# Later remainder terms in a three-term float32r product: a conv + RG-LRU layer on one core

## The chip, the core and the metric

The kernel runs on one core of a Trainium2 chip. The engines that matter are TensorE (PE, the matmuls; its weight loads are listed as PEld), VectorE (DVE), ScalarE (ACT), GpSimd (POOL, which here issues the transfers that add into their destination) and SyncE (SP, which issues the plain transfers). The metric is the device time of one execution in microseconds (us). Before the change the median of three runs is 729.47 us (728.41 to 730.4).

## The reference

One layer of a hybrid decoder: 1024 tokens of 1024 channels, float32.

```python
mod = silu(c) @ mod_w + mod_b
shift, scale, gate = split(mod, 3)
h = rmsnorm(x, norm_g) * (1 + scale) + shift
cv, cg, cs, lx, ls = split(h @ w_in)            # five blocks of 1024 columns

v = cv * sigmoid(cg)                            # conv group
v = causal_depthwise_conv(v, dw_w, dw_b)        # 31 taps
v = silu(layernorm(v, cln_g, cln_b))
y_conv = (v @ pw2_w + pw2_b) * silu(cs)

xs = causal_depthwise_conv(lx, sc_w, sc_b)      # lru group, 4 taps
r, i = sigmoid(xs @ wr + br), sigmoid(xs @ wi + bi)   # 8 heads of 128
a = exp(-8 * r * softplus(-lam))
hs = linear_scan(a, sqrt(1 - a**2) * (i * xs))
y_lru = hs * silu(ls)

x = x + (1 + gate) * (concat([y_conv, y_lru]) @ w_out)
out = rmsnorm(x, final_g)
```

The parts that the change touches are the product `v @ pw2_w`, and the product with `w_out`: its upper half takes `y_conv`, its lower half `y_lru`.

## The kernel before

**Layout.** Channels lie on the 128 partitions and the 1024 tokens on the free axis, so a 1024 x 1024 operand is eight tiles of 128 x 1024. A matmul takes a 128 x 128 block of weights and 512 tokens.

**A product of three terms.** The matmuls run in float32r, which keeps fewer bits than float32. So each operand is split into a high part, rounded to float32r, and a remainder, and a product is the sum of three matmuls: H, high weights by high data; X, high weights by the remainder of the data; W, the remainder of the weights by high data. In names, `h` and `l` mark the two: `yha0` and `yla0`, `whiout1` and `wloout1`, `whi46` and `wlo46`. In `mm_k` and in `product` (inside `pair_products`) the three terms stand side by side for every k block: H, X, W of block 0, then of block 1, and so on, in one operation of three (or six) matmuls that asks for all four operands.

**How remainders are made.** Those of the data come mostly from VectorE (a subtraction, L405). Those of weights come from VectorE, or by `remainder`: ScalarE writes minus the high part, and a transfer issued by POOL adds the original to it from DRAM. `remainder` makes `wlo46` and `wlo47`, the remainders of the weights of the last two lru tiles, as it makes `wlopw20`, `wloout0` and `wloout1`.

**The lower half of the output, lru pairs and tiles.** `w_out`'s lower half by `y_lru` is computed first, while the conv group is still in its LayerNorm: `lru_pair` computes output tiles 0 to 5 in pairs (PSUM tiles `lp`, `lx`, `ly`; pair 2 is number 44 and 45), and the last two tiles are plain ones, number 46 and 47 (`ps46`, `ps47`), by `mm_k` over eight k blocks. Each tile is scaled by the gate into `acc0` to `acc7`; then POOL issues a transfer that adds it onto a copy of x in DRAM (`accd0` to `accd7`). Later SP loads `accd` back as `fin`, onto which the upper half of the output is added.

**The pairs of the conv group.** `pw2` and the upper half of `w_out` go two output tiles at a time: pairs 0 to 3 of each, named `pw2_0` to `out_3`. A pair is computed with seven products of half size (`pair_products`), called `1 z 2 y 3 s 4`, of sums and differences of the quarters. Product `1` is the quarter A11 by B11 (data `vha`, `vla` or `yha`, `yla` in PSUM tile `x`), `z` is A12 by B21 (`vhb`, `vlb`, tile `z`), `y` takes T1 and `4` takes T4. The data's quarters are split by `quarters`, half on ScalarE and half on VectorE. The evacuations of the PSUM tiles go to `yc` (pw2) and `fin` (out).

**Order.** All instructions are put in order by `Plan`, ahead of the run. Each operation has an engine, an assumed cost, a priority number and the operations that it must wait for, by the buffers that it reads and writes. `Plan.order` plays time forward: whenever an engine is free, it takes the ready operation with the smallest priority. So a change of what one operation reads can move many others on every engine. The order is then fixed; on the chip an engine runs its list in that order and stops at the first instruction whose inputs are not there. Most tiles of 128 x 1024 come from one pool of 47 buffers (`big`); an instruction that takes a buffer waits until the last use of the one before is over, a transfer out of it included.

Of the kernel before, what the change touches and what calls it, by code (L numbers as in the profile page):

```python
# [16 lines left out]
T = 1024  # L17
# [81 lines left out]
LWO = 0.5  # L99
LRV = ()  # L100
# [233 lines left out]
def hymba_layer(ctx: ExitStack, tc: tile.TileContext, xT, vecs, mod_w, w_first, w_in,  # L334
# [162 lines left out]
    def w_slice(s, k, nk, p_load, p_prep, first_load=(), eng="POOL", late=()):  # L497
# [6 lines left out]
        if eng == "DMA":  # L504
            remainder(p_prep, cut(lo), cut(hi), lambda: wsrc(s)[:, c, :], n, keys(hi), keys(lo))
# [11 lines left out]
    def weights(s, after=(), n=None, eng=None, where=None, late=()):  # L517
# [3 lines left out]
        w_slice(s, 0, KT, n - 2.5, n - 1.4, after, eng, late)  # L521

    def mm_k(prio, ps, s, xh, xl, k, cols, off=0, first=0, final=KT - 1, after=()):
        wh, wl = whi[s], wlo[s]
        at = LK.index(k) if s[0] == "lru" else k

        def emit():
            for lhs, rhs, last in ((wh, xh, 0), (wh, xl, 0), (wl, xh, 1)):
                for a, b in cols:
# [3 lines left out]
                              stop=(k == final and bool(last)), skip_group_check=True)  # L533
        n = sum(b - a for a, b in cols)
        rd = [(wh, at), (wl, at)]
        wr = []
        for a, b in cols:
            rd += halves(xh[k], a, b) + halves(xl[k], a, b)
            wr += halves(ps, a - off, b - off)
        return S.op("PE", 3 * sum((b - a + 32) / 2400 for a, b in cols), emit, prio, rd, wr, after=after, columns=3 * n)  # L540
# [145 lines left out]
    def pair_products(name, n, w, sets, use, orders=(ORDER7,), apart=0):  # L686
# [7 lines left out]
        def product(a, b, ps, start):  # L694
            (wh, wl), xs, made = w[a], sets[b], products[name, c]
            for j, (bh, bl) in enumerate(xs):
                def emit(j=j, bh=bh, bl=bl):
                    for lhs, rhs, t in ((wh, bh, 0), (wh, bl, 1), (wl, bh, 2)):
                        pe.matmul(half(ps, 0)(), half(*lhs)()[:, j * P:j * P + P], half(*rhs)(),  # L699
                                  start=start and j == 0 and t == 0,  # L700
                                  stop=j == KT // 2 - 1 and t == 2, skip_group_check=True)
                o = S.op("PE", 3 * (H + 32) / 2400, emit, n + 0.15 * q, [wh, wl, bh, bl],
                         [ps], columns=3 * H)
                made.append(o)
                if j == 0:
                    ops.append(o)

        for order in orders:
# [18 lines left out]
            n += apart  # L727

    def rstd(prio, sqs, a, e, ps, o, after=(), warm=(), idle=None):
# [27 lines left out]
        S.op("DVE", 0.2, lambda: dve.reciprocal(rs()[:, :nb], sd()[:, :nb]), prio, [sd], [rs])  # L757
# [986 lines left out]
```

## Time and profile before

| | |
|---|---|
| median of 3 runs | 729.47 us (728.41 to 730.4) |
| profiled execution, its own time | 730.56 us |
| its span in the profile | 728.7 us |
| granted TensorE clock, mean | 0.996 |
| TensorE busy | 718.4 us (99%), 3274 matmuls |
| VectorE, ScalarE, POOL busy | 616.9, 481.7, 171.0 us |

The span runs from the first to the last instruction that the profile lists; the execution's own time holds 1.9 us more. Rows of a timeline have the start from the beginning of the span, the length, the engine, the line of the kernel, the operation with output and inputs (buffer numbers are left out, so `vlb` stands for `vlb0` to `vlb3`), and in brackets the engine's idle time before it and what ended it. Matmuls overlap: the length shown of one with 512 columns is 0.39 us, though the next may start 0.23 us after it. So a stop of TensorE is read from the starts.

Of the work named here, the LayerNorm of the conv group and lru pair 2 lie at about 500 to 540 us, `ps46` and `ps47` up to 560, the four pairs of pw2 from 560 to 640, the four pairs of out from 634 on, the final norm and the stores after 702.

### The profile page before, as it was taken

What the parts mean: (1) busy time and instruction counts of PE and PEld (TensorE: products, weight loads), DVE (VectorE), ACT (ScalarE), POOL (GpSimd) and SP (SyncE); (2) the same over time, 40 slices, a digit from 0 to 9 for tenths busy, and PEclk for the clock granted to TensorE, in tenths of its full rate; (3) what the DMA queues carried; (4) which work ended last, traced back from release to release, by engine and by line L of the source; (5) the groups of instructions that cost most, each with busy time, mean ns of one, the idle gap of its engine ahead of it and who ended that gap; (6) DMA issues with size and microseconds to landing.
All of it is one profiled execution on the core that took longest, in us unless ns stands there. A gap on an engine that the chain in (4) does not pass through costs nothing.

```text
span 728.7 us, 9085 instructions
## 1 busy us (share of the span) xinstructions
PE 718.4 (99%) x3274; PEld 597.2 (82%) x3274; DVE 616.9 (85%) x848; ACT 481.7 (66%) x615; POOL 171.0 (23%) x172
## 2 busy tenths in 40 slices
PE   9999999999999999999999999999999999999996
PEld 8888888888888888888888888878878788878885
DVE  7999999899689998688499995999788666999646
ACT  7650679555689857957949779858874345755322
POOL 0035223443434230233220220211101101110003
PEclk9999999999999999999999999999999999999998
DMA  8945338768899997899998687998936955784006
GB/s 340 407 158 167 51 112 234 189 119 199 192 217 206 263 234 196 183 224 211 192 246 259 125 175 173 255 249 229 226 44 140 250 122 138 216 224 159 8 15 216
DMA packets 46059, 137.80 MB, mean 189 GB/s; under 512 B 5200, under 2 KB 15824, under 8 KB 45904
## 3 DMA queue, kind: packets, MB, share of 16 engines
q0 software_dynamic: 20016, 54.84, 41.8%
q1 hardware_dynamic: 24992, 81.48, 32.2%
q10 hardware_dynamic: 1008, 0.92, 0.4%
q8 instruction: 25, 0.41, 0.2%
q14 instruction: 18, 0.15, 0.1%
HBM read 79.37 MB, written 21.50 MB: 138 GB/s over the span
## 4 chain that ended last, share of the span: by engine, by line
PE 81%; issue 6%; DVE 5%; ACT 4%; DMA 2%; POOL 1%; DVEq 0%; POOLq 0%; ACTq 0%
PE ps L530 49%; PE xout L699 5%; PE first L826 5%; PE xpw L699 5%; PE ypw L699 3%; PE gate L1246 2%; PE y L674 2%; PE lp L530 1%; DMA wloout<-in_w_out_dram 1%; PE zpw L699 1%; DMA accd<-acc 1%; PE zout L699 1%; PE lx L1378 1%; ACT L386 1%; PE yout L699 1%
## 5 line engine op out<-in xcount | busy, mean ns | idle before, releaser
L530 PE MATMUL ps<-ul,whi 128*128 128x512 f32 x576 | 177.4, 389 | 0.0
L530 PE MATMUL ps<-uh,whi 128*128 128x512 f32 x576 | 177.4, 389 | 0.0
L530 PE MATMUL ps<-uh,wlo 128*128 128x512 f32 x576 | 177.2, 389 | 0.0
L530 PEld LDWEIGHTS ps<-ul,whi 128*128 128x128 f32 x576 | 108.1, 188 | 22.5
L530 PEld LDWEIGHTS ps<-uh,wlo 128*128 128x128 f32 x576 | 108.1, 188 | 22.5
L530 PEld LDWEIGHTS ps<-uh,whi 128*128 128x128 f32 x576 | 108.0, 188 | 22.3
L378 ACT CAST whi<-raw 128x1024 fp32r<-128x1024 f32 (+1 forms) x44 | 45.1, 1032 | 46.1 <-PE ps L530 28.4
L410 POOL DMA_DIRECT2D es<-cq x45 | 40.6, 902 | 129.8 <-ACT cq L386 89.6
L405 POOL TENSOR_TENSOR wlo<-raw,whi 128x1024 fp32r<-128x1024 f32 x16 | 41.8, 2618 | 88.9 <-ACT whi L378 88.8
L386 ACT ACT_TABLE_LOAD x45 | 57.7, 1283 | 5.4 <-issue 1.8
L397 DVE SCALAR_TENSOR_TENSOR cacc<-v,V,cacc 128x511 f32<-128x511 f32 (+14 forms) x75 | 55.5, 740 | 0.5
L397 DVE SCALAR_TENSOR_TENSOR caccs<-v,V,caccs 128x511 f32<-128x511 f32 (+6 forms) x70 | 52.0, 742 | 2.2 <-ACT caccs L386 1.1
L397 DVE SCALAR_TENSOR_TENSOR caccs<-c,wsum,caccs 128x511 f32<-128x511 f32 (+6 forms) x70 | 51.9, 742 | 0.8
L410 POOL DMA_DIRECT2D oo<-co x39 | 36.8, 975 | 43.0 <-issue 12.8
L386 ACT ACTIVATE cq<-v,V 128x511 f32<-128x511 f32 (+14 forms) x45 | 31.7, 707 | 0.0
L397 DVE SCALAR_TENSOR_TENSOR xs<-ps,V,xs 128x1023 f32<-128x1023 f32 (+2 forms) x24 | 30.6, 1274 | 0.0
L405 DVE TENSOR_TENSOR wlo<-raw,whi 128x1024 fp32r<-128x1024 f32 x20 | 24.4, 1218 | 6.5 <-ACT whi L378 6.4
L386 ACT ACTIVATE cq<-c,wsum 128x512 f32<-128x512 f32 x42 | 29.6, 711 | 0.0
L397 DVE SCALAR_TENSOR_TENSOR modw<-modw,sc 128x1024 f32<-128x1024 f32 x23 | 29.5, 1285 | 0.0
L386 ACT ACTIVATE co<-v,V 128x510 f32<-128x510 f32 (+12 forms) x39 | 26.9, 705 | 0.0
L386 ACT ACTIVATE finsq<-fin 128x512 f32<-128x512 f32 (+2 forms) x14 | 7.8, 569 | 26.7 <-DVE fin L397 13.5
L405 POOL TENSOR_TENSOR o<-fin,bc 128x256 f32<-128x256 f32 (+1 forms) x8 | 7.8, 997 | 70.6 <-ACT bc L378 70.6
(413 smaller groups left out, 1590.6 us busy)
## 6 DMA issues: line engine op xcount, KB each, us to landing
raw<-in_w_in_dram SPq DMA_DIRECT2D x36, 512.0 KB, 5.8
modw<-in_mod_w_dram SPq DMA_DIRECT2D x24, 512.0 KB, 9.1
scsd<-scs SPq DMA_DIRECT2D x8, 512.0 KB, 4.0
raw<-in_w_out_dram SPq DMA_DIRECT2D x8, 512.0 KB, 7.5
accd<-acc POOLq DMA_DIRECT2D x8, 512.0 KB, 6.9
rawpw<-in_pw_dram SPq DMA_DIRECT2D x8, 512.0 KB, 4.5
scsr<-scsd SPq DMA_DIRECT2D x8, 512.0 KB, 5.2
rawout<-in_w_out_dram SPq DMA_DIRECT2D x8, 512.0 KB, 3.7
```

The source lines that it names most:

```text
L378: act.copy(out(), in_())
L386: act.activation(out=out(), in_=in_(), func=func, **kw)
L397: dve.scalar_tensor_tensor(out=out(), in0=in0(), scalar=scalar, in1=in1(), op0=op0, op1=op1, accum_out=accum)
L405: lambda: e.tensor_tensor(out=out(), in0=a(), in1=b(), op=op), prio, r, w,
L410: return S.op("POOL", ISSUE, lambda: pool.dma_start(out(), a(), accum_op=ALU.add), prio, r, w, lag=RATE * n / T, after=after, flight=flight)
L530: pe.matmul(ps()[:, a - off:b - off], k3(lhs)()[:, at, :], rhs[k]()[:, a:b], start=(k == first and lhs is wh and rhs is xh and (a - off) % ...
L674: pe.matmul(to(), half(*lhs)()[:, j * P:j * P + P], half(*rhs)()[:, c0:c1], start=a == "S1" and j == 0 and t == 0, stop=j == KT // 2 - 1 a ...
L699: pe.matmul(half(ps, 0)(), half(*lhs)()[:, j * P:j * P + P], half(*rhs)(), start=start and j == 0 and t == 0, stop=j == KT // 2 - 1 and t ...
L826: pe.matmul(ps()[:, a - off:b - off], fw_part(lhs, k, i * P, i * P + P)(), rhs()[:, a:b], start=k == 0 and lhs is wh and rhs is xh, stop=k ...
L1246: pe.matmul(ps()[:, c0:c1], lhs()[:, j, :], rhs()[:, c0:c1], start=st == 0, stop=st == 2)
L1378: pe.matmul(half(ps, h)(), lhs()[:, o:o + P], half(*rhs)(), start=begin and j == 0 and t == 0, stop=j == NJ - 1 and t == 2, skip_group_che ...
```

## The change

The terms H, X and W of a product become letters of a group, and a product can be given as several groups that run one after the other over all k blocks. An operation of a group asks only for the operands that its terms read.

- `TERMS`: product `1` of pw2 pairs 1 to 3 and of all four out pairs runs as H and X of every block first, then W of every block. Products `1` and `z` of pw2 pair 0 run as H and W first, then X.
- `SLOTT`: tiles 46 and 47 run as H and X over their eight blocks, then W.
- `LLATE`: the remainders `wlo46` and `wlo47` (ScalarE's copy, and with it POOL's transfer) may be made only once the operation noted as the start of slot 45 (the first of product `2` of lru pair 2) is over.

Four more settings come with it at values that change nothing: `FINP` and `FINQ` (with -0.5 and 0.0, the number that stood there), `BCLATE` (False), `BEHIND` (0) and `LTERMS` (empty); the code that they switch is left out below. After's lines are numbered higher than before's by 8 to 18, so that L405 is L413 and L699 is L717.

```diff
+TERMS = {**{("pw2_0", c): ("HW", "X") for c in "1z"}, **{(f"out_{p}", "1"): ("HX", "W") for p in (0, 1, 2, 3)}, **{(f"pw2_{p}", "1"): ("HX", "W") for p in (1, 2, 3)}}
+LLATE = 45
+SLOTT = {46: ("HX", "W"), 47: ("HX", "W")}
...
-    def remainder(prio, lo, hi, src, n, rk, wk, sk=(), reserve=0):
-        ACT(prio, lo, lambda: hi().bitcast(F32), AF.Copy, n, scale=-1.0, r=rk, w=wk, reserve=reserve)
+    def remainder(prio, lo, hi, src, n, rk, wk, sk=(), reserve=0, after=()):
+        ACT(prio, lo, lambda: hi().bitcast(F32), AF.Copy, n, scale=-1.0, r=rk, w=wk, reserve=reserve,
+            after=after)
         ADD(prio, lo, src, n, r=[*wk, *sk], w=wk, flight=LAND)
...
+    def mm_k(prio, ps, s, xh, xl, k, cols, off=0, first=0, final=KT - 1, after=(), group="HXW", end=True):
         wh, wl = whi[s], wlo[s]
         at = LK.index(k) if s[0] == "lru" else k
+        terms = [{"H": (wh, xh), "X": (wh, xl), "W": (wl, xh)}[t] for t in group]
...
-        rd = [(wh, at), (wl, at)]
+        rd = [(wh, at)] * ("H" in group or "X" in group) + [(wl, at)] * ("W" in group)
...
         def product(a, b, ps, start):
             (wh, wl), xs, made = w[a], sets[b], products[name, c]
-            for j, (bh, bl) in enumerate(xs):
...
+            groups = TERMS.get((name, c), ("HXW",))
+            order = [(g, j) for g in groups for j in range(len(xs))]
+            for at, (g, j) in enumerate(order):
+                bh, bl = xs[j]
+                terms = [{"H": (wh, bh), "X": (wh, bl), "W": (wl, bh)}[t] for t in g]
...
+                rd = list(dict.fromkeys(k for t in terms for k in t))
+                o = S.op("PE", len(g) * (H + 32) / 2400, emit, n + 0.15 * q, rd, [ps],
+                         columns=len(g) * H)
...
-                weights(s, n=n - LWO, eng="DVE" if s[1] in LRV else "DMA", where=LWB)
+                weights(s, n=n - LWO, eng="DVE" if s[1] in LRV else "DMA", where=LWB,
+                        later=[started[LLATE]] if LLATE else [])
...
-        for k in range(KT):
-            o = mm_k(n, ps, s, xh, xl, k, FULL)
-            if k == 0:
+        groups = SLOTT.get(n, ("HXW",))
+        for gr, k in [(gr, k) for gr in groups for k in range(KT)]:
+            o = mm_k(n, ps, s, xh, xl, k, FULL, group=gr, end=gr == groups[-1])
+            if k == 0 and gr == groups[0]:
```

No engine gets more or fewer instructions. What the order makes of it is shown at three places.

**Place 1, around lru pair 2.** POOL's queue, before and after (`accd2` and `accd3` add tiles 2 and 3 onto DRAM):

```order
L410 DMA accd2_120<-acc2_4075 128x1024
L410 DMA wlo46_4163<-in_w_out_dram 128x1024
L410 DMA wlo47_4193<-in_w_out_dram 128x1024
L410 DMA accd3_121<-acc3_4138 128x1024
L410 DMA accd4_122<-acc4_4260 128x1024
```
```order
L418 DMA accd2_120<-acc2_4075 128x1024
L418 DMA accd3_121<-acc3_4138 128x1024
L418 DMA wlo46_4271<-in_w_out_dram 128x1024
L418 DMA wlo47_4286<-in_w_out_dram 128x1024
L418 DMA accd4_122<-acc4_4248 128x1024
```
`accd3` moved ahead of the two remainders, which now stand directly ahead of `accd4`. ScalarE in the same stretch, first before, where `wlo46` and `wlo47` are made ahead of the LayerNorm's SiLUs (`cr0` is the first of eight), then after, from the last SiLU (`c7`) on:

```order
L378 CAST whi46_4160<-raw46_4113 128x1024
L386 ACTIVATE wlo46_4163<-whi46_4160 128x1024
L386 ACTIVATE sd-1_0_4168<-lnbc_4150,eps_t_91 128x8
L378 CAST whi47_4187<-raw47_4128 128x1024
L386 ACTIVATE wlo47_4193<-whi47_4187 128x1024
L386 ACT_TABLE_LOAD
L386 ACTIVATE cr0_3941<-cr0_3941,V_80 128x1024
```
```order
L394 ACTIVATE c7_3062<-c7_3062,V_80 128x1024
L394 ACTIVATE wlo46_4271<-whi46_4160 128x1024
L394 ACTIVATE acc4_4248<-ly2_4145,gate1_95 128x512
L394 ACTIVATE wlo47_4286<-whi47_4184 128x1024
L386 CAST vha0_4294<-cr0_3941 128x512
```
Both copies moved behind the eight SiLUs, ahead of the split of the conv operand (`vha0`).

**Place 2, product z of pw2 pair 0.** TensorE before and after, its twelve matmuls (before's last five of them, after's last six):

```order
L699 MATMUL zpw2_0_4558<-vlb2_4427,whipw20_4415 128x512
L699 MATMUL zpw2_0_4558<-vhb2_4393,wlopw20_4429 128x512
L699 MATMUL zpw2_0_4558<-vhb3_4404,whipw20_4415 128x512
L699 MATMUL zpw2_0_4558<-vlb3_4548,whipw20_4415 128x512
L699 MATMUL zpw2_0_4558<-vhb3_4404,wlopw20_4429 128x512
```
```order
L717 MATMUL zpw2_0_4558<-vhb3_4449,whipw20_4381 128x512
L717 MATMUL zpw2_0_4558<-vhb3_4449,wlopw20_4396 128x512
L717 MATMUL zpw2_0_4558<-vlb0_4375,whipw20_4381 128x512
L717 MATMUL zpw2_0_4558<-vlb1_4427,whipw20_4381 128x512
L717 MATMUL zpw2_0_4558<-vlb2_4457,whipw20_4381 128x512
L717 MATMUL zpw2_0_4558<-vlb3_4535,whipw20_4381 128x512
```
The reading of `vlb3` moved from the eleventh to the twelfth place. VectorE, which makes `vlb3` (`acc7` is the evacuation of `ps47`):

```order
L405 TENSOR_TENSOR l34pw20_4523<-rawpw20_0_4342,h34pw20_4505 128x1024
L405 TENSOR_TENSOR vlc3_4525<-vt3_4493,vhc3_4515 128x1024
L405 TENSOR_TENSOR vu3_4448<-c7_3062,vt3_4493 128x512
L419 TENSOR_SCALAR acc7_4538<-ps47_4451,gate1_95 128x1024
L405 TENSOR_TENSOR vlb3_4548<-c7_3062,vhb3_4404 128x1024
```
```order
L413 TENSOR_TENSOR vu3_4413<-c7_3062,vt3_4488 128x512
L413 TENSOR_TENSOR l34pw20_4512<-rawpw20_1_4350,h34pw20_4500 128x1024
L413 TENSOR_TENSOR vlc3_4520<-vt3_4488,vhc3_4507 128x1024
L413 TENSOR_TENSOR l34pw20_4529<-rawpw20_0_4300,h34pw20_4514 128x1024
L413 TENSOR_TENSOR vlb3_4535<-c7_3062,vhb3_4449 128x1024
L427 TENSOR_SCALAR acc7_4546<-ps47_4452,gate1_95 128x1024
```
`vlb3` moved ahead of `acc7`.

**Place 3, product 1 of out pair 1.** TensorE from its first matmul before, and from its sixth after:

```order
L699 MATMUL xout_1_5230<-yha0_4774,whiout1_5142 128x512
L699 MATMUL xout_1_5230<-yla0_4785,whiout1_5142 128x512
L699 MATMUL xout_1_5230<-yha0_4774,wloout1_5153 128x512
L699 MATMUL xout_1_5230<-yha1_4957,whiout1_5142 128x512
L699 MATMUL xout_1_5230<-yla1_4980,whiout1_5142 128x512
L699 MATMUL xout_1_5230<-yha1_4957,wloout1_5153 128x512
```
```order
L717 MATMUL xout_1_5231<-yla2_5067,whiout1_5173 128x512
L717 MATMUL xout_1_5231<-yha3_5115,whiout1_5173 128x512
L717 MATMUL xout_1_5231<-yla3_5121,whiout1_5173 128x512
L717 MATMUL yout_1_5246<-yha0_4774,h34out1_5220 128x512
L717 MATMUL yout_1_5246<-yla0_4785,h34out1_5220 128x512
L717 MATMUL yout_1_5246<-yha0_4774,l34out1_5234 128x512
L717 MATMUL yout_1_5246<-yha1_4954,h34out1_5220 128x512
L717 MATMUL yout_1_5246<-yla1_4980,h34out1_5220 128x512
L717 MATMUL yout_1_5246<-yha1_4954,l34out1_5234 128x512
L717 MATMUL xout_1_5231<-yha0_4774,wloout1_5180 128x512
L717 MATMUL xout_1_5231<-yha1_4954,wloout1_5180 128x512
```
The reading of `wloout1` moved from the third place to the fifteenth, behind six matmuls of `yout_1`; three of `yout_0` that followed the product stand ahead of it now. ScalarE, which makes `wloout1`'s first part, has changed too: it made `whiout1` and `wloout1` ahead of `yhb3` (the high part of the last `b` quarter of the operand), and makes them directly behind it now.

More of the change, by code (lines that the diff above doesn't have):

```diff
@@ L515, in w_bufs, with weights @@
         wlo[s] = S.buf("big" if where else "wlo", f"wlo{n}", F32R, KT)
-    def weights(s, after=(), n=None, eng=None, where=None, late=()):
+    def weights(s, after=(), n=None, eng=None, where=None, late=(), later=()):
         n = number[s] if n is None else n
@@ L520, in weights @@
         w_bufs(s, where)
-        w_slice(s, 0, KT, n - 2.5, n - 1.4, after, eng, late)
-    def mm_k(prio, ps, s, xh, xl, k, cols, off=0, first=0, final=KT - 1, after=()):
+        w_slice(s, 0, KT, n - 2.5, n - 1.4, after, eng, late, later)
+    def mm_k(prio, ps, s, xh, xl, k, cols, off=0, first=0, final=KT - 1, after=(), group="HXW", end=True):
         wh, wl = whi[s], wlo[s]
         at = LK.index(k) if s[0] == "lru" else k
+        terms = [{"H": (wh, xh), "X": (wh, xl), "W": (wl, xh)}[t] for t in group]
         def emit():
-            for lhs, rhs, last in ((wh, xh, 0), (wh, xl, 0), (wl, xh, 1)):
+            for i, (lhs, rhs) in enumerate(terms):
                 for a, b in cols:
@@ L1387, in lru_pair @@
             if c == "p":
-                for k in rest:
-                    o = mm_k(n + g, p0, s0, yh, yl, k, FULL, first=rest[0])
-                    ops.setdefault(c, o)
+                groups = LTERMS.get(p, ("HXW",))
+                for gr in groups:
+                    for k in rest:
+                        o = mm_k(n + g, p0, s0, yh, yl, k, FULL, first=rest[0], group=gr,
+                                 end=gr == groups[-1])
+                        ops.setdefault(c, o)
             elif c == "q":
@@ L1686, in hymba_layer @@
         norm(z, a, e)
+    for o in scalings[END[1][0]][len(scalings[END[1][0]]) - BEHIND:]:
+        S.hold(o, inverse[END[2][0]])
     S.run()
```

51 lines of the change are left out of this document (31 added, 20 removed).

## The prediction

> **What bounds the kernel now.** I read the page's busy times first, then TensorE's waits in the last third of the span, then busy time by stretch, and only then the chain of waits, which says who is behind each wait.
>
> ```profile
> PE 718.4 (99%) x3274; PEld 597.2 (82%) x3274; DVE 616.9 (85%) x848; ACT 481.7 (66%) x615; POOL 171.0 (23%) x172
> ```
> TensorE is the bound: 718.4 of 728.7 us. The number of matmuls stays, so the change can only win what TensorE idles, and only where it idles inside the changed stretch. Every matmul has a weight load of its own (x3274 on both), so another order of the same matmuls saves or adds no load.
>
> The waits of TensorE from 480 us on (line, waited for, total, times, longest):
>
> ```profile
> PE finbc L748 <- DVE rs65.7_0_5820 L757: 0.9, 1, 0.9
> PE xout L699 <- DMA wloout<-in_w_out_dram: 0.8, 1, 0.8
> PE lx L1378 <- DVE acc L397: 0.5, 1, 0.5
> PE zpw L699 <- DVE vlb L405: 0.4, 1, 0.4
> ```
> The first lies in the final norm, which keeps its order. The other three lie in the changed products. These figures start only when the modelled end of the last matmul has passed, so they are too small: the loss is read from starts. Two rows of busy time by stretch (us, then each engine's busy time and count, granted clock, DMA share, GB/s):
>
> ```profile
> 530.00:533.00 3.00, 2.47 (x11) 1.75 (x10) 2.48 (x5) 1.43 (x3) 0.00 (x0) 1.00 0.00 0
> 566.00:636.00 70.00, 70.00 (x310) 57.95 (x309) 48.71 (x68) 38.02 (x51) 7.84 (x9) 1.00 0.70 176
> ```
> In 566 to 636 TensorE never stops: 70.00 / 310 = 0.226 us from one matmul to the next. That is the pace against which a gap is a loss. The clock is 1.00 in both, so no gap is a throttle.
>
> **The change part by part.** Nothing is added or removed on any engine; every instruction is moved. So each term is a stall of before that goes, or a new one. I walked the new orders through with the durations of before; all times below are in before's clock.
>
> *A, lru pair 2.* TensorE at the product that waits, and then the chain of waits ahead of it (start, length, what):
>
> ```profile
> 530.64 0.39 PE L530 MATMUL ly<-yl,whi 128*128 128x512 f32 x1
> 530.87 0.39 PE L530 MATMUL ly<-yh,wlo 128*128 128x512 f32 x1
> 531.79 0.50 PE L1378 MATMUL lx<-yhs,lsh 128*128 128x512 f32 x1 [0.53 <-DVE acc L397]
> 532.13 0.39 PE L1378 MATMUL lx<-yls,lsh 128*128 128x512 f32 x1
> ```
> ```profile
> 515.02 0.86 POOL wlo L410
> 518.05 0.83 POOL wlo L410
> 520.71 8.32 DMA accd<-acc
> 529.12 0.06 DVE vt L405
> 531.08 0.67 DVE acc L397
> ```
> The start after 530.87 should be at 531.10 and is at 531.79: 0.69 lost, and the next start comes 0.34 later instead of 0.226, another 0.11: 0.80 us. I use that 0.11 as the price of each restart below. Behind it stands VectorE, which sat before `vt` until `accd3` had landed (it needs the buffer that `acc3` leaves); and `accd3` was issued only at 520.71, behind `wlo46` and `wlo47` in POOL's queue. ScalarE makes those two early as well:
>
> ```profile
> 510.25 1.06 ACT L386 ACTIVATE wlo<-whi 128x1024 fp32r<-128x1024 f32 x1
> 527.68 1.23 ACT L386 ACTIVATE c<-c,V 128x1024 f32<-128x1024 f32 x1
> 529.12 0.69 DVE L405 TENSOR_TENSOR vt<-c,cr 128x512 f32<-128x512 f32 x1 [2.04 <-DMA accd<-acc]
> ```
> Now `accd3` is ahead and its source is ready some 1.1 us earlier, since one 1.06 us copy is no longer ahead of the LayerNorm's SiLUs: issue about 519.2. Even at 8.32 us it lands by 527.5, when `vt` is due at 527.1. The 2.04 us wait goes, the evacuation of `lx2` ends about 530.2 and its next product is due at 532.69: A goes whole, -0.80.
>
> The two remainders cost ScalarE 2 x 1.06 us after the SiLUs, with the evacuation of `ly2` into `acc4` between them (ending 529.1, for a product due at 530.0), and POOL two issues at about 528.9 and 530.5. Their readers, the W terms of `ps46` and `ps47`, come at about 544.5 and 555.4, against landings by 539 even at 8.32 us: no cost there. What is late next is `accd4`, which now stands behind them at about 531.9. In the stretch 530 to 533 no DMA moves a byte (0.00, 0 GB/s), so the three have the engines to themselves. Rows that price them (KB each, median us to landing; below, the extremes for all eight):
>
> ```profile
> accd<-acc POOLq DMA_DIRECT2D x5, 512.0 KB, 5.2
> wlo<-in_w_out_dram POOLq DMA_DIRECT2D x3, 512.0 KB, 8.5
> DMA to landing us min/median/max: 3.5/7.2/13.0
> ```
> 5.2 gives 537.1, 8.5 gives 540.4. With two others in front in the same queue I take 539.3 (one transfer's spacing in before is about 3 us: 515.02, 518.05). VectorE, whose `vla2` needs the buffer of `acc4`, then idles about 3 us there, plus some on `vla0`, in place of the 2.04 and the 2.59 below: about as much. The Trainium skill, page "DMA: Bandwidth & Descriptors" (Anatomy of one DMA), fits 2.0 us plus bytes over 436e3, an estimate of 3.2 us for 512 KB; the 3.5 us minimum comes near, the 5.2 us median doesn't, and by its figure this wait would be 4 us shorter and B's margin wider.
>
> *B, the z product of pw2 pair 0.*
>
> ```profile
> 564.57 0.39 PE L699 MATMUL zpw<-vhb,whipw 128*128 128x512 f32 x1
> 565.39 0.50 PE L699 MATMUL zpw<-vlb,whipw 128*128 128x512 f32 x1 [0.43 <-DVE vlb L405]
> 548.50 1.23 DVE L405 TENSOR_TENSOR vlb<-c,vhb 128x1024 fp32r<-128x1024 f32 x1 [2.59 <-DMA accd<-acc]
> 562.93 1.28 DVE L419 TENSOR_SCALAR acc<-ps,gate 128x1024 f32<-128x1024 f32 x1
> 564.12 1.21 DVE L405 TENSOR_TENSOR vlb<-c,vhb 128x1024 fp32r<-128x1024 f32 x1
> ```
> Loss: 0.82 - 0.226 + 0.11 = 0.70. Putting the X terms last moves the reading of `vlb3` back by one matmul only, 0.23. The larger part is VectorE's order: `vlb3` now stands ahead of `acc7`, whose slot is 564.12 - 562.93 = 1.19. So it ends near 563.6 instead of 565.33, if VectorE is otherwise as far as before (its lost time is the same, above). The last X term is due at 564.2. B goes, -0.70, with a margin of 0.6.
>
> *pw2 pairs 1 to 3.* The remainders of their weights move to the end of the first product. TensorE never waited there; nothing to win, and nothing to lose while VectorE is busy 48.71 of 70.00: 0.
>
> *C, into the out products.*
>
> ```profile
> 636.51 0.39 PE L699 MATMUL xout<-yha,wloout 128*128 128x512 f32 x1
> 636.88 0.50 PE L699 MATMUL xpw<-vhT,hlpw 128*128 128x512 f32 x1
> 634.41 0.68 DVE L405 TENSOR_TENSOR yla<-yc,yha 128x512 fp32r<-128x512 f32 x1
> 636.15 0.68 DVE L405 TENSOR_TENSOR yc<-xpw,yc 128x512 f32<-128x512 f32 x1
> ```
> 0.37 - 0.226 + 0.11 = 0.26 lost on the evacuation of `xpw2_3`. In VectorE's new order `yla3` (635.01 - 634.41 = 0.60, to the row after it) stands behind that evacuation, which ends near 636.4 for a need at 636.74: -0.26.
>
> *D, the first product of out pair 1.*
>
> ```profile
> 649.49 0.39 PE L699 MATMUL xout<-yla,whiout 128*128 128x512 f32 x1
> 650.67 0.50 PE L699 MATMUL xout<-yha,wloout 128*128 128x512 f32 x1 [0.79 <-DMA wloout<-in_w_out_dram]
> 641.37 9.25 DMA wloout<-in_w_out_dram
> 637.15 0.88 POOL L410 DMA_DIRECT2D ylc<-yt  x1 [5.34 <-DVE yc L405]
> 639.90 1.06 ACT L386 ACTIVATE wloout<-whiout 128x1024 fp32r<-128x1024 f32 x1
> 641.19 1.05 ACT L378 CAST yhb<-yc 128x1024 fp32r<-128x1024 f32 x1 [0.22 <-DVE yc L397]
> DMA to landing us min/median/max: 5.2/7.2/9.3
> ```
> Loss: 1.18 - 0.226 + 0.11 = 1.06. The first W term now comes 15 matmuls later in TensorE's queue (six more H and X terms, six of `yout_1`, three of `yout_0` that moved ahead), and C's gain comes off: due at 652.8. Against it, ScalarE makes `yhb3` ahead of `whiout1` and `wloout1`, so the copy ends near 644.6 and POOL issues near 645.0. Between 5.2 (650.2) and 9.25 (654.3) I take 5.2, since `ylc1` has landed by then: -1.06, with 2.6 in hand. At 9.25 TensorE would wait 1.5 instead. The Trainium skill, same page (Issuing engines are not separate DMA queues), says that transfers of SP and POOL share the 16 engines and interleave; the 9.25 beside `ylc1` and loads of `fin`, against 5.2 for the other `wloout` that went by POOL, agrees, and by it the row to take hangs on what is under way beside it.
>
> *New: the evacuation of `fin1`.* VectorE has two more instructions ahead of it than before:
>
> ```profile
> 663.47 1.43 DVE L397 SCALAR_TENSOR_TENSOR fin<-xout,gate,fin 128x512 f32<-128x512 f32 x2
> 664.62 0.39 PE L699 MATMUL xout<-yhT,hlout 128*128 128x512 f32 x1
> ```
> Half of the 1.43 ends at 664.2, for the product at 664.62. One of the two (a fin of 0.7) was right behind it, the other is a 0.6 us combination; VectorE gains some 0.7 of the 1.3 back from a wait that it had before. It ends near 664.75: a stall of 0.0 to 0.6, I take 0.24. After it the same hand walk finds margins of 0.4 and more, and the order from about 702 us on is unchanged.
>
> **Sum:** -0.80 - 0.70 - 0.26 - 1.06 + 0.24 = -2.58 us. Against the profiled execution (730.56, of which 728.7 are the span) that is 727.98; that execution lies 1.09 above the median of 729.47, from which I forecast 726.9.
>
> **The rivals.**
>
> *The stalls move.* Several margins are under 0.7 us (the evacuation into `acc5` 0.26, B 0.6, C 0.34, `fin1` already gone). If `accd4` lands at 540.4, by the 8.5 row, VectorE is 1.1 later, and B comes back with 0.5 + 0.11; if `wloout1` takes 9.25, D comes back as 1.5. Both: -2.58 + 0.61 + 1.61 = -0.36, 729.1; one of them: 727.5 to 728.5. For it: VectorE is busy nearly throughout from 533 to 565, so it can't catch up. Against it: A and C stand on other waits, and the DMA engines are idle when `accd4` starts.
>
> *Slower: `accd4` is late by much.* One mechanism: `accd4` and its two predecessors in POOL's queue. Each us beyond 539.9 goes straight through VectorE to `zpw2_0`. At the longest landing of its kind, 13.0, it comes at 544.9: a stall of 5.0 + 0.11, and -2.58 + 5.1 = +2.5, 732.0. It turns the kernel slower from a landing at 542.4 on (10.5 us), and by over 0.3% from 544.6 on. For it: two 512 KB accumulates right in front, of the 8.5 kind. Against it: the 13.0 fell elsewhere, and here three in a row would have to take the pace of a full machine with 0 GB/s beside them.
>
> *It doesn't do what it says.* If the waits that I read are only the last of two (another input just as late behind each), nothing moves: 729.5. Against: the chain of A runs through six rows, and B's `vlb3` is the last thing that VectorE does there.
>
> **How the numbers follow.** 0.3% is 2.19 us, about what a measurement of this kernel can tell from no change. The forecast's own case (all four stalls gone, small new ones of 0 to 0.7 together) gets 0.58 and reaches from 726.4 to 727.7; about 0.47 of it lies beyond 0.3%, 0.11 within. The moved stalls get 0.27, all within. The late `accd4` gets 0.11, slower. No effect gets 0.04, within. So faster 0.47, same 0.42, slower 0.11. The range for 8 in 10 runs from 726.2 (every stall of the zone, 2.9, with a little for the run) to 729.8, which leaves out the slower rival and little else.
>
> **What would show it.** TensorE's waits after 480 us should list `finbc` and no `lx`, `zpw` or `xout<-DMA wloout`; in its place perhaps a short `xout` wait on a `fin`. VectorE's wait on `accd<-acc` before `vt` should be gone, and one of about 3 us stand before a `vla`, near 536 to 539. `accd3` should be issued near 519 and the two `wlo` near 529 and 530.5. `wloout1` should be issued near 645 and land before 652. The forecast is wrong if `zpw2_0` still waits on `vlb`, if `xout_1` waits on `wloout`, or if waits on evacuations appear in 566 to 636.

## The result, and the profile after

| | before | after |
|---|---|---|
| median of 13 runs each | 729.26 us | 728.27 us (726.9 to 728.77) |
| ratio after to before | | 0.9983, 95% interval 0.9975 to 0.9991 |
| profiled execution, its own time | 730.56 us | 728.60 us |
| its span | 728.7 us | 726.8 us |

The ratio makes the changed kernel 0.17% faster, 1.2 us (0.7 to 1.8); the two medians by themselves differ by 1.0. The forecast was 2.6 us. A second comparison on another occasion gave 0.9975 (0.9966 to 0.9983), 1.8 us.

A line of the kernel before has a higher number in the changed kernel: L699 is L717, and from about L740 on the distance is 22 or more, so that L748 is L770, L826 is L848 and L1378 is L1400.

TensorE's busy time in the profile after, and then all of its waits from 480 us on:

```profile
PE 717.4 (99%) x3274; PEld 596.6 (82%) x3274; DVE 616.5 (85%) x848; ACT 481.0 (66%) x615; POOL 170.9 (24%) x172
```
```profile
PE finbc L770 <- DVE rs65.7_0_5820 L779: 0.9, 1, 0.9
```
Of the four waits of this list before, only the one of the final norm is left. `lx`, `zpw` and `xout` are gone from it, and the starts no longer show the short loss on `xpw2_3`. POOL's queue around lru pair 2, and VectorE there and at `zpw2_0` (start, length, engine, line, what; in brackets the idle time before it):

```profile
520.14 0.88 POOL L418 DMA_DIRECT2D accd<-acc  x1 [7.18 <-ACT acc L394]
529.68 0.87 POOL L418 DMA_DIRECT2D wlo<-in_w_out_dram  x1 [8.67 <-ACT wlo L394]
531.20 0.89 POOL L418 DMA_DIRECT2D wlo<-in_w_out_dram  x1 [0.65 <-ACT wlo L394]
532.87 0.88 POOL L418 DMA_DIRECT2D accd<-acc  x1 [0.78 <-DVE acc L405]
```
```profile
540.43 0.69 DVE L413 TENSOR_TENSOR vla<-cr,vha 128x512 fp32r<-128x512 f32 x1 [3.37 <-DMA accd<-acc]
563.49 1.21 DVE L413 TENSOR_TENSOR vlb<-c,vhb 128x1024 fp32r<-128x1024 f32 x1
564.62 1.27 DVE L427 TENSOR_SCALAR acc<-ps,gate 128x1024 f32<-128x1024 f32 x1
```
`accd3` goes out at 520.14, the two remainders at 529.68 and 531.20, `accd4` behind them at 532.87 (this execution runs some 0.8 us late from its start on, see below). VectorE's wait for `accd3` is gone, and a new one of 3.37 us for `accd4` stands before `vla2`. `vlb3`, now ahead of `acc7`, ends at 564.70; its reader, the last matmul of the z product, starts at 565.10 without a stop. At `wloout1` (POOL's issue; issue to landing of the transfers into `wloout` from 600 to 660 us) and at `fin1`:

```profile
644.19 0.86 POOL L418 DMA_DIRECT2D wloout<-in_w_out_dram  x1 [8.93 <-PE zout L717]
DMA to landing us min/median/max: 5.8/5.8/5.9
```
```profile
663.70 0.39 PE L717 MATMUL xout<-yhc,l34out 128*128 128x512 f32 x1
663.99 0.50 PE L717 MATMUL xout<-yhT,hlout 128*128 128x512 f32 x1
664.32 0.40 PE L717 MATMUL xout<-ylT,hlout 128*128 128x512 f32 x1
```
`wloout1` takes 5.9 us at most, instead of 9.25, so it lands by 650.1, and its W terms start at 652.1: 2 us in hand. At `fin1` 0.29 - 0.226 + 0.11 = 0.17 us are lost.

So between 480 and 702 us TensorE lost 2.98 us in the profile before (the four stalls, 2.82, and 0.16 near 691) and 0.17 in the profile after: 2.8 us less, a little more than forecast. (Two gaps of 0.09 near 512 and 515, which every profile has, are left out.) Yet the spans differ by 1.9 only. The rest went at the start, which the change does not touch; TensorE's starts there, and VectorE's wait from the list of waits up to 60 us:

```profile
11.05 0.86 PE L848 MATMUL first<-uh,flo 128*128 128x512 f32 x3
12.72 0.96 PE L848 MATMUL first<-ul,fhi 128*128 128x512 f32 x3 [0.81 <-DVE ul L405]
```
```profile
DVE modw L405 <- DMA modw<-in_mod_w_dram: 2.1, 1, 2.1
```
Here TensorE stops for 1 us in the first stage: VectorE had waited 2.1 us for a load of `modw` and made `ul` late. The profile before has no such stop. And two profiles do not tell why the medians differ by only 1.0.

### The profile page after: what moved, and what is told of

Read it like the earlier page. It is cut to its first block, busy times and chain, and to the rows that moved or that the text cites. A ratio compares the mean times of both kernels' runs of the same rounds, so it can differ in the third digit from the quotient of the medians.

```text
span 726.8 us, 9080 instructions
## 1 busy us (share of the span) xinstructions
PE 717.4 (99%) x3274; PEld 596.6 (82%) x3274; DVE 616.5 (85%) x848; ACT 481.0 (66%) x615; POOL 170.9 (24%) x172
## 4 chain that ended last, share of the span: by engine, by line
PE 88%; ACT 4%; DVE 3%; issue 2%; DMA 1%; SPq 0%; DVEq 0%; ACTq 0%
PE ps L541 50%; PE xout L717 6%; PE xpw L717 6%; PE first L848 5%; PE ypw L717 3%; PE gate L1268 2%; PE lp L541 2%; PE lx L1400 2%; PE y L687 2%; PE zout L717 1%; PE zpw L717 1%; PE ly L541 1%; PE lx L541 1%; PE yout L717 1%; PE lp L1400 1%
## 5 line engine op out<-in xcount | busy, mean ns | idle before, releaser
L413 POOL TENSOR_TENSOR wlo<-raw,whi 128x1024 fp32r<-128x1024 f32 x16 | 41.6, 2606 | 89.8 <-ACT whi L386 89.6
L405 DVE SCALAR_TENSOR_TENSOR cacc<-v,V,cacc 128x511 f32<-128x511 f32 (+14 forms) x75 | 55.6, 741 | 0.5
L405 DVE SCALAR_TENSOR_TENSOR caccs<-v,V,caccs 128x511 f32<-128x511 f32 (+6 forms) x70 | 52.0, 743 | 2.2 <-ACT caccs L394 1.1
L405 DVE SCALAR_TENSOR_TENSOR caccs<-c,wsum,caccs 128x511 f32<-128x511 f32 (+6 forms) x70 | 52.0, 742 | 0.8
L405 DVE SCALAR_TENSOR_TENSOR modw<-modw,sc 128x1024 f32<-128x1024 f32 x23 | 29.5, 1286 | 2.1 <-DMA modw<-in_mod_w_dram 2.1
L405 DVE SCALAR_TENSOR_TENSOR xs<-ps,V,xs 128x1023 f32<-128x1023 f32 (+2 forms) x24 | 30.6, 1275 | 0.0
L413 DVE TENSOR_TENSOR wlo<-raw,whi 128x1024 fp32r<-128x1024 f32 x20 | 24.4, 1219 | 6.5 <-ACT whi L386 6.3
L413 POOL TENSOR_TENSOR o<-fin,bc 128x256 f32<-128x256 f32 (+1 forms) x8 | 7.8, 996 | 68.1 <-ACT bc L386 68.1
```

What stands on the lines that cost most here:

```text
L405: dve.scalar_tensor_tensor(out=out(), in0=in0(), scalar=scalar, in1=in1(), op0=op0, op1=op1, accum_out=accum)
L413: lambda: e.tensor_tensor(out=out(), in0=a(), in1=b(), op=op), prio, r, w,
```

## The experiments

For each profiled execution I read the same places by starts, as the prediction does: A lru pair 2, B `zpw2_0`, C `xpw2_3`, D `wloout1`. A ratio is always to the kernel before, with its 95% interval.

**More profiles of the same two kernels.** Edit: none.

> The kernel before once more, unchanged, for a second profiled execution. Theory 1 (the four stalls of TensorE are about as long in every execution, and what the changed kernel gives less than the 2.6 us is lost elsewhere): starts of matmuls again lose about 0.80, 0.70, 0.26 and 1.06 us at the four places, 2.8 us in all, within 0.3. Theory 2 (the stalls hang on landings and differ from one execution to the next, and the first profile caught long ones): the sum is nearer to 1.3, mainly by the first and the last, which wait on a transfer. Theory 3 (executions differ by their first 60 us, where TensorE waits on loads): up to 1 us more or less before 60 us, the four stalls unchanged.

> A third profiled execution of the kernel before. Theory 1: 2.8 us at the four places, within 0.3. Theory 2: another sum than in the other two, between 0.5 and 2.8. Theory 3: 2.8 at the four places, and a loss before 60 us that differs from the other executions.

> The changed kernel once more, unchanged. Theory 1 with margins that hold: TensorE loses under 0.3 us between 480 and 702 us, at the product of fin1 only. Rival (the small margins fail in other executions): 0.5 us or more lost at zpw2_0, at the evacuation into acc5, at ylb3 or at wloout1. Theory 3: 0.7 to 1.2 us lost near 12 us as in its first profile if that is a lasting disadvantage of this program, none if it is chance.

> A third profiled execution of the changed kernel. As for the second: under 0.3 us lost between 480 and 702 us if the margins hold, 0.5 or more if one fails; the loss before 60 us tells chance from a lasting disadvantage.

The fourth profile of the changed kernel belongs to its second timed comparison, further down. Lost time in us, and the execution's own time; "rest" is that time less the sum:

```
                 A     B     C     D     near 691  fin1   sum    own time   rest
before, first    0.80  0.70  0.26  1.06  0.16      -      2.98   730.56    727.58
before, second   0.54  0.32  0.26  0.94  0.16      -      2.22   729.60    727.38
before, third    0.92  0.57  0.26  0     0.16      -      1.91   729.96    728.05
after, first     0     0     0     0     0         0.17   0.17   728.60    728.43
after, second    0     0.28  0     0     0         0.18   0.46   728.36    727.90
after, third     0     1.06  0     0     0         0.18   1.24   729.64    728.40
after, fourth    0     0     0     0     0         0.16   0.16   727.61    727.45
```
The stalls aren't fixed. C, which waits on VectorE's own order, is 0.26 each time. A, B and D, which hang on landings, change from one execution to the next; D is not there at all in the third. Its rows, TensorE and POOL:

```profile
650.01 0.39 PE L699 MATMUL xout<-yla,whiout 128*128 128x512 f32 x1
650.24 0.39 PE L699 MATMUL xout<-yha,wloout 128*128 128x512 f32 x1
640.67 0.86 POOL L410 DMA_DIRECT2D wloout<-in_w_out_dram  x1 [2.17 <-PE xpw L699]
```
`wloout1` was issued 0.7 us earlier than in the first profile while TensorE was 0.5 us later. Its landing took 9.4 us, as long as the 9.25 there, so these 1.2 us are all of D. In the second execution the landing took 10.1 us, and the list of waits has D again:

```profile
PE xout L699 <- DMA wloout<-in_w_out_dram: 0.7, 1, 0.7
```
And B comes back in the changed kernel, in two of four. VectorE before `vla2` in the second, third and fourth execution:

```profile
540.09 0.69 DVE L413 TENSOR_TENSOR vla<-cr,vha 128x512 fp32r<-128x512 f32 x1 [3.86 <-DMA accd<-acc]
```
```profile
541.10 0.69 DVE L413 TENSOR_TENSOR vla<-cr,vha 128x512 fp32r<-128x512 f32 x1 [4.65 <-DMA accd<-acc]
```
```profile
539.50 0.69 DVE L413 TENSOR_TENSOR vla<-cr,vha 128x512 fp32r<-128x512 f32 x1 [3.43 <-DMA accd<-acc]
```
Waits of 3.37 and 3.43 us for `accd4` cost TensorE nothing, 3.86 costs 0.28, 4.65 costs 1.06. The 0.28 is a gap of 0.17 and the 0.11 of a restart, so the waits that cost begin at about 3.7 us. Between the two waits that cost, 0.79 us apart, the loss grows by 0.78: VectorE catches up with nothing between the two places. In the third execution TensorE stops there:

```profile
563.80 0.84 PE L717 MATMUL zpw<-vlb,whipw 128*128 128x512 f32 x3
565.43 0.50 PE L717 MATMUL zpw<-vlb,whipw 128*128 128x512 f32 x1 [0.79 <-DVE vlb L413]
```
The mean sum is 2.37 before (three) and 0.51 after (four): 1.86 less, near what the timed runs say (1.2 and 1.8). The rest, 727.4 to 728.4, differs within each kernel by as much as between them; the 1 us at the start is in one of the seven. So theory 1 (the same 2.8 us each time) falls: the four places lost 2.06 and 1.75 in the second and third execution. Theory 2 holds in kind, though not with a sum near 1.3 in the second. Of theory 3 it holds that the start differs from one execution to the next, not that the four stalls stay. The stop at the start is no lasting disadvantage of the changed kernel. And the 0.28 of its second execution lies between what the theory and its rival had expected, the 1.06 of the third is the rival's.

**Without the later remainders.** Product splits stay, `wlo46` and `wlo47` are made where they were.

```diff
-LLATE = 45
+LLATE = 0
```


> Only the later remainders are undone: wlo46 and wlo47 are made where they were, ahead of accd3; all split products stay. Theory 1 (holding wlo46 and wlo47 back wins the first stall and pays for it at accd4): the stall of lru pair 2 is back with 0.5 to 0.9 us; VectorE no longer waits 3 us for accd4, and vlb3, which stands ahead of acc7 here too, is in time: nothing lost at zpw2_0. The stalls on the evacuation of xpw2_3 and on wloout1 stay away. So 1.4 to 1.8 us under the kernel before, ratio 0.9976 to 0.9981: as fast as the changed kernel. Theory 2 (the later remainders are worth their 0.8 us): ratio about 0.9994, 0.8 us slower than the changed kernel.

Measured: 0.9971 (0.996 to 0.9982). Its profile, VectorE:

```profile
528.99 0.69 DVE L413 TENSOR_TENSOR vt<-c,cr 128x512 f32<-128x512 f32 x1 [2.12 <-DMA accd<-acc]
541.11 0.69 DVE L413 TENSOR_TENSOR vlT<-vu,vhT 128x512 fp32r<-128x512 f32 x1 [1.49 <-DMA accd<-acc]
```
A is back with 0.90; the wait for `accd4` is 1.49 us and comes later; nothing is lost at B, C and D. The total lost is 1.20, with 0.19 at `fin1` and 0.11 more in lru pair 2. That is theory 1, with a ratio a little better than its 0.9976 to 0.9981: holding the remainders back moves a wait of VectorE from `accd3` to `accd4`. B's cure doesn't come from it either, since `vlb3` stands ahead of `acc7` here as well.

**Only the later remainders.**

```diff
-TERMS = {**{("pw2_0", c): ("HW", "X") for c in "1z"}, ...
+TERMS = {}
-SLOTT = {46: ("HX", "W"), 47: ("HX", "W")}
+SLOTT = {}
```


> Only the later remainders; every product keeps its terms side by side. Theory 1: the stall of lru pair 2 is gone; VectorE waits 3 to 4.7 us for accd4, and vlb3 is late again by 0.2 to 1.2 us at zpw2_0; the stalls on xpw2_3 (0.26) and on wloout1 (0 to 1.06) stay. Together 0.3 to 1.0 us under the kernel before, ratio 0.9986 to 0.9996. Theory 2: the first and second stall both gone, 1.4 us, ratio 0.9981.

Measured: 1.0009 (1.0 to 1.0018), no gain at all. A went, B lost 0.28 and C 0.25, and D was not there in its profile. Both theories had expected a gain. `vlb3` stands ahead of `acc7` here too, so the later remainders bring that order by themselves, as the splits do; B's loss is that of a late VectorE. And a stall came that neither theory had, TensorE in lru pair 2 and the evacuation that it waits for:

```profile
534.18 0.50 PE L1400 MATMUL lx<-yhs,whi 128*128 128x512 f32 x1 [1.44 <-DVE acc L405]
533.38 0.74 DVE L405 SCALAR_TENSOR_TENSOR acc<-lx,gate,acc 128x512 f32<-128x512 f32 x1
```
1.60 + 0.11 = 1.71 us, on the evacuation into `acc5`. In the changed kernel eight matmuls of `ps46` (H and X terms, which don't ask for `wlo46`) stand just ahead of this product; here no term of `ps46` can, since each of its operations asks for a remainder that is late. That reading rests on the orders alone, so a further run put the split of the two tiles back.

**The later remainders and the split of tiles 46 and 47.** `TERMS` is empty, the rest as in the changed kernel.

```diff
-TERMS = {**{("pw2_0", c): ("HW", "X") for c in "1z"}, ...
+TERMS = {}
```


> The later remainders together with the split of tiles 46 and 47; the products of the pairs keep their terms side by side. Theory (with the remainders alone, TensorE stopped 1.7 us at the evacuation into acc5, because no term of ps46 could come ahead; the split of the two tiles lets H and X terms do so): no loss over 0.3 us at the evacuation into acc5; B 0 to 1.1 us by the wait for accd4, C 0.26 and D 0 to 1.06 stay; 1.0 to 1.7 us faster than with the remainders alone, ratio 0.9985 to 0.9997. Rival (the stall at acc5 comes from the other late work on ScalarE and VectorE): 1 us or more lost there again, ratio 1.0 or more.

Measured: 0.9989 (0.9978 to 0.9999). TensorE at the place of the stall:

```profile
534.87 0.62 PE L541 MATMUL ps<-yl,whi 128*128 128x512 f32 x2
535.33 0.40 PE L1400 MATMUL lx<-yhs,whi 128*128 128x512 f32 x1
```
Eight matmuls of `ps46` now stand ahead of the product, and nothing is lost there. B lost 0.19, C 0.24, D 0.71. The split of tiles 46 and 47 is what makes the later remainders bearable, and with them it gives about what the out pairs give alone (below, 0.9989 too). The split of the two tiles without the later remainders was not run.

**Only the out pairs.**

```diff
-TERMS = {**{("pw2_0", c): ("HW", "X") for c in "1z"}, ...
+TERMS = {(f"out_{p}", "1"): ("HX", "W") for p in (0, 1, 2, 3)}
-LLATE = 45
-SLOTT = {46: ("HX", "W"), 47: ("HX", "W")}
+LLATE = 0
+SLOTT = {}
```


> Only product 1 of the four out pairs is split, the rest as before. The W terms of out pair 1 come eight matmuls after the place of the first in the kernel before, which is about 651.5 us in its clock, against landings of wloout1 near 650.6. Theory (the split alone takes the wait on wloout1 away, and it is there in some executions only): no wait on wloout1, the other three stalls as before; 0.3 to 1.0 us under the kernel before, ratio 0.9986 to 0.9996. Rival (the place of the copy on ScalarE matters, and it is the order there that the other splits bring): a wait on wloout1 stays or is at most halved, ratio 0.9995 or more.

Measured: 0.9989 (0.9979 to 0.9998). A lost 0.69, B 0.82, C 0.26, D nothing:

```profile
651.46 0.84 PE L717 MATMUL xout<-yha,wloout 128*128 128x512 f32 x3
640.86 0.86 POOL L418 DMA_DIRECT2D wloout<-in_w_out_dram  x1 [2.50 <-ACT wloout L394]
```
The first W term runs at 651.46, 10.6 us after the issue, more than the longest landing of `wloout1` seen (10.1). So the split is enough for D by this sum; the copy's other place on ScalarE is not needed. The profile itself does not show the cure: the landing took 8.8 us here, to 649.7, and the third place of the product, at 650.10, would have been in time as well. The stronger evidence is the count. All nine profiles of kernels with this split lose nothing at D; of the five without it (three of the kernel before, the two experiments above with `TERMS` empty) three lose 0.71 to 1.06. C, on the other hand, stays here and with `TERMS` empty, and is gone in every profile with the pw2 pairs split: its cure hangs on those. Which of the pw2 pairs is needed for it, or for B, no run tells.

**The remainders behind `accd4`.** `evacuated[4]` are the last evacuations into `acc4`.

```diff
...
+                evacuated[m] = [S.writer[t, 0], S.writer[t, 1]]
...
-                        later=[started[LLATE]] if LLATE else [])
+                        later=evacuated[4])
```


> The changed kernel with wlo46 and wlo47 held until the last evacuation into acc4, so that POOL issues accd4 ahead of both of them instead of behind. Theory 1 (the wait for accd4, 3.4 to 4.7 us, is what brings the stall at zpw2_0 back): accd4 lands within 5.5 us of its issue, VectorE's wait for it shrinks under 1.5 us, nothing is lost at zpw2_0, and the kernel is 0.4 to 0.8 us faster than the changed one: ratio to the kernel before 0.9968 to 0.9978. Rival (another transfer in the row, accd5 or accd6, takes its place, since the same three transfers share POOL's queue): VectorE waits 2 us or more for accd5 or accd6, the loss at zpw2_0 stays at 0.3 to 1 us, ratio 0.998 to 0.999.

Measured: 0.9976 (0.9966 to 0.9987). POOL's queue, then ScalarE and VectorE:

```profile
535.64 0.86 POOL L418 DMA_DIRECT2D accd<-acc  x1 [15.79 <-DVE acc L405]
536.88 1.83 POOL L418 DMA_DIRECT2D wlo<-in_w_out_dram  x2 [0.37 <-ACT wlo L394]
541.19 0.87 POOL L418 DMA_DIRECT2D accd<-acc  x1 [2.49 <-ACT acc L394]
```
```profile
549.81 1.05 ACT L386 CAST vhc<-vt 128x1024 fp32r<-128x1024 f32 x1 [5.46 <-DMA accd<-acc]
```
```profile
550.89 1.23 DVE L413 TENSOR_TENSOR vlc<-vt,vhc 128x1024 fp32r<-128x1024 f32 x1 [4.90 <-ACT vhc L386]
```
No wait for `accd4` is left, and now `accd5` is the late one: behind the two remainders it takes 549.81 - 541.19 = 8.6 us, ScalarE waits 5.46 us for its buffer and VectorE 4.90 for ScalarE. 0.25 us are lost at B, and 0.51 at the evacuation into `acc5`, the margin that the prediction had at 0.26. So the rival has the wait right, while the ratio lies in theory 1's range, with an interval that reaches into the rival's. Neither loss can be put down to `accd5` alone, because the order changed as well. VectorE's list, then TensorE's at the evacuation into `acc5`:

```profile
562.59 1.28 DVE L427 TENSOR_SCALAR acc<-ps,gate 128x1024 f32<-128x1024 f32 x1
563.78 1.21 DVE L413 TENSOR_TENSOR vlb<-c,vhb 128x1024 fp32r<-128x1024 f32 x1
```
```profile
533.33 0.62 PE L541 MATMUL ps<-yh,whi 128*128 128x512 f32 x2
533.78 0.61 PE L541 MATMUL ps<-yl,whi 128*128 128x512 f32 x2
534.64 0.50 PE L1400 MATMUL lx<-yhs,whi 128*128 128x512 f32 x1 [0.24 <-DVE acc L405]
```
`acc7` stands ahead of `vlb3` again, as before the change, and only four matmuls of `ps46` stand ahead of the product that waits, instead of eight.

**One remainder late instead of two**, with the changed kernel and the one without the later remainders beside it.

```diff
-                        later=[started[LLATE]] if LLATE else [])
+                        later=[started[LLATE]] if s[1] == 7 else [])
```


> The changed kernel with only wlo47 held back; wlo46 is made where it was before the change. POOL's queue has accd3 behind wlo46 and ahead of wlo47, and accd4 behind wlo47 alone. Theory (each stall is paid by the transfers directly ahead in POOL's queue): accd3 is issued about 1 us earlier than before the change or more and VectorE waits under 0.8 us for it, so the stall of lru pair 2 goes; accd4 lands over 1 us earlier than in the changed kernel, nothing is lost at zpw2_0. Only the 0.2 us at fin1 stay: 0.4 to 0.8 us faster than the changed kernel in the same job, ratio to the kernel before 0.9962 to 0.9975. Rival (one remainder ahead is as bad as two): one of the two stalls is there with 0.5 us or more, and the time is that of the changed kernel within 0.3 us.

> The changed kernel, unchanged, beside the two others on the same chip. Ratio 0.9975 to 0.9991 as in its first comparison, 1.2 us under the kernel before. In the profile 0.2 to 1.3 us lost from 480 to 702 us, most of it at zpw2_0 where VectorE waited over 3.6 us for accd4.

> The changed kernel without the later remainders, again, beside the changed kernel. Theory 1 (the later remainders win and lose about the same): within 0.5 us of the changed kernel in this job, either side; the stall of lru pair 2 there with 0.5 to 0.9 us, none at zpw2_0. Theory 2 (they cost): 0.5 us or more faster than the changed kernel, as the first comparison had it (0.9971 against 0.9983).

Measured side by side: 0.9975 (0.9965 to 0.9985) with one late, 0.9975 (0.9966 to 0.9983) for the changed kernel, 0.9985 (0.9976 to 0.9995) without. With one late, POOL and VectorE:

```profile
514.12 0.86 POOL L418 DMA_DIRECT2D wlo<-in_w_out_dram  x1 [1.89 <-issue]
518.98 0.88 POOL L418 DMA_DIRECT2D accd<-acc  x1 [3.99 <-ACT acc L394]
529.57 0.88 POOL L418 DMA_DIRECT2D wlo<-in_w_out_dram  x1 [9.71 <-ACT wlo L394]
535.25 0.89 POOL L418 DMA_DIRECT2D accd<-acc  x1 [4.81 <-DVE acc L405]
```
```profile
540.55 0.69 DVE L413 TENSOR_TENSOR vlT<-vu,vhT 128x512 fp32r<-128x512 f32 x1 [1.44 <-DMA accd<-acc]
```
Both VectorE waits are cured or short: none for `accd3`, 1.44 us for `accd4`, and only 0.29 us are lost by TensorE (0.18 at `fin1`, 0.11 in pair 2). But `accd4` lands no earlier than in the changed kernel; it goes out later and in 5.2 us, and VectorE has more to do before it needs the buffer. The gain expected over the changed kernel did not come: its own profile in this comparison is the fourth of the table, with 0.16 lost.

The kernel without the later remainders missed an expectation: A, expected with 0.5 to 0.9 us, is not there in its second profile. Its first profile, with ScalarE at `whi47` and POOL at `accd3`, and then its second, with VectorE's wait for `accd3` too:

```profile
514.44 1.06 ACT L386 CAST whi<-raw 128x1024 fp32r<-128x1024 f32 x1 [2.71 <-DMA raw<-in_w_out_dram]
520.58 0.89 POOL L418 DMA_DIRECT2D accd<-acc  x1 [1.66 <-ACT acc L394]
```
```profile
513.52 1.04 ACT L386 CAST whi<-raw 128x1024 fp32r<-128x1024 f32 x1 [1.83 <-DMA raw<-in_w_out_dram]
519.62 0.89 POOL L418 DMA_DIRECT2D accd<-acc  x1 [2.41 <-ACT acc L394]
528.03 0.69 DVE L413 TENSOR_TENSOR vt<-c,cr 128x512 f32<-128x512 f32 x1 [1.20 <-DMA accd<-acc]
```
The load of `raw47` landed 0.9 us earlier, and with it ScalarE's `acc3` and the issue of `accd3` came earlier by as much. VectorE's wait was 1.20 us instead of 2.12, and TensorE lost nothing in place of 0.90. Waits of 1.76, 1.92, 2.04 and 2.12 us lost 0.54, 0.69, 0.80 and 0.90 in the other profiles: each the wait less 1.33 to 1.35, plus 0.11. So A too is absent from some executions without any cure.

The two comparisons put the kernel without later remainders ahead of the changed one once and behind it once, with intervals that overlap; no difference between the three is shown, and so no gain from the later remainders where the products are split.

## Why the prediction was right or wrong

- **Direction and mechanism: right.** TensorE was the bound, nothing was added, and A to D are gone from the first profile after, though B came back in two of the next three. What the prediction named as signs came: `accd3` near 519, the remainders near 529 and 530.5, a wait of about 3 us before a `vla` (3.37, forecast near 536 to 539), a `wloout1` issued at 644.2, and a short `xout` wait on a `fin`.
- **The sum: too large, and this is the step that failed.** "-0.80 - 0.70 - 0.26 - 1.06 + 0.24 = -2.58" was read off one execution and then subtracted from the median. That execution lay 1.09 us above the median, and the prediction said so without asking why. The further profiles answer a part of it: it had the largest stalls of the three (2.98 against 2.22 and 1.91), 0.6 above their mean. Taken from the execution itself, the sum gave 727.98, against 728.27 measured; taken from the median it counted time that the median execution, as far as three profiles tell, doesn't have in full.
- **Term D, -1.06: mis-sized.** It measured 1.06, 0.94 and 0 in three executions, mean 0.67. The cure was right (with the out pairs split no profile has it), and so was taking a landing of the short kind, 5.2 us, which measured 5.9 in the first profile after.
- **Term B, -0.70 with a margin of 0.6: right in half of the executions.** VectorE's order was the cause, as said. Before, B was 0.70, 0.32 and 0.57; after 0, 0.28, 1.06 and 0. Net that is about -0.2 and not -0.70. The rival that names `accd4` had the mechanism and nearly the point: stalls beyond a landing at 539.9, with each us going straight through. The landing of `accd4` took 7.4 and 7.5 us where nothing was lost, 7.9 where 0.28 was, 8.7 where 1.06 was; the prediction took 7.4 and a margin to 8.0. What was wrong is the chance: it was treated as a case of its own, and it is a spread between executions.
- **Term A, -0.80: right in kind**, 0.54 to 0.92 before, 0 after. The queue's part in it was misread: POOL had sent `wlo47` off and sat idle for ScalarE's `acc3` when `accd3` went out (row below). What the two remainders ahead cost `accd3` is its landing, 8.32 us against 5.20 in the first profile after; the prediction counted with 8.32 for both. It also did not see that the cure depends on the split of tiles 46 and 47: with the later remainders alone a new stall of 1.71 us stands in the same pair, and with the two tiles split it goes. And the stall is absent in one execution of two without the later remainders but with the splits.

```profile
520.71 0.89 POOL L410 DMA_DIRECT2D accd<-acc  x1 [1.82 <-ACT acc L386]
```
- **The prices of `accd4`: one row misread.** The "3.5/7.2/13.0" are not extremes of eight transfers but of 25, for every transfer that reads or writes `accd`: the 13.0 is a copy of x into it and the 3.5 a load of `fin`, both issued by SP. The eight accumulates of POOL took 5.1 to 9.2 in that profile. So the 3.5 us minimum that the prediction names is no accumulate, and the slower rival, which needed 10.5 us, had no row of its kind. In the four executions `accd4` took 8.7 us at most.
- **Term C, -0.26, and `fin1`, +0.24: right**, 0.26 each time before and 0.16 to 0.18 after.
- **pw2 pairs 1 to 3 at nothing: right**, no loss from 566 to 630 us in any profile.
- **Against 0.3%**: the change is measured at 0.17%, and 0.25% the second time, within the bound that the prediction set. It had 0.42 for that and 0.47 for more, so the outcome that it held likeliest did not come.

## What to carry to other kernels

A stall read from one profiled execution is a sample: look where that execution lies against the median, subtract from its own time, and expect a stall that waits on a transfer to be smaller, or absent, in others. Here the one that waits on another engine's order was the same each time. A transfer that is moved in a queue was paid here by the next one behind it: the wait went from `accd3` to `accd4`, and with `accd4` ahead on to `accd5`, and it cost TensorE only beyond what VectorE had in hand. Holding back an operand needs other work that does not ask for it: the later remainders alone won nothing, and with those two tiles split they did. Beside the splits of the products, though, they added nothing that these runs show.

## What was not expected of the hardware

- Executions of one program lose between 0 and 1.06 us at one and the same place (D), with the same order on every engine, by an issue or a landing that is about 1 us earlier or later. The first stage differs by up to 1 us as well.
- After each stop at A to D and `fin1`, the matmul behind the one that had waited starts 0.34 us after it instead of 0.226, even where the wait was under 0.1 us (`fin1`).
- `accd3` and `accd4`, 512 KB accumulates issued by POOL, landed in 5.0 to 5.5 us where none of the remainders was under way, in 6.9 beside one, and in 7.4 to 8.7 beside two. The Trainium skill, page "DMA: Bandwidth & Descriptors" (Issuing engines are not separate DMA queues), has all transfers interleave on the same 16 engines; these lengths agree. The fit of the Trainium skill on the same page (Anatomy of one DMA), 2.0 us plus bytes over 436e3, gives an estimated 3.2 us for 512 KB. No `accd` between 500 and 560 us in these profiles reached it; the shortest there took 5.0.
